# Shorter product waits in the first block's LayerNorm chain, and another start and rate for the second block's convolution, in a one-core encoder block on Trainium2

## The chip, the cores and the metric

The kernel runs on one core of one Trainium2 chip. Its time is the device time of one execution, in microseconds (us). Before the change the median of three runs is 2229.48 us, the lowest 2222.62 and the highest 2231.29. About 0.5%, some 11 us, is what a measurement of this kernel can tell from no change.

## The reference, cut to what matters

One layer of a streaming encoder works on 2048 tokens of 1024 channels. An input projection makes the input of a pooling branch, a pair for a gated linear unit (GLU) and two gates. The branch that this change concerns takes the GLU's output through a causal convolution of width 31 per channel, a LayerNorm over its 512 channels, a swish and a projection; the pooling branch takes means over trailing windows.

```python
def trailing_mean_minus_self(u, window):        # windows 2, 4, 8, 16 by group of 128 channels
    ...
    return (mean - uf).astype(u.dtype)

def pool_mixer(u, pool_w, pool_scale, w_pool_out):
    ...                                         # a 128x128 map for each group
    return mixed @ w_pool_out

def conformer_conv(glu_in, conv_w, conv_b, ln_g, ln_b, w_conv_out):
    a, gate = jnp.split(glu_in, 2, axis=-1)
    v = a * jax.nn.sigmoid(gate)
    v = lax.conv_general_dilated(v, rhs, ...) + conv_b
    v = layernorm(v, ln_g, ln_b)
    v = jax.nn.silu(v)
    return v @ w_conv_out

    merged = jax.nn.sigmoid(g_a) * branch_a + jax.nn.sigmoid(g_b) * branch_b
    x = x + rmsnorm(merged @ w_o[l], norm_mix_post[l])
    h = rmsnorm(x, norm_mlp_pre[l])
    f = jnp.square(jax.nn.relu(h @ w_up[l])) @ w_down[l]
```

## The kernel before, in words

The tokens are worked in two blocks of 1024 (`b` is 0 for block one and 1 for block two). A tile is 128 partitions by 1024 elements, 512 KB. Each large matrix product is split into a high and a low part in fp32r, so that a product of two operands takes three matmul passes, and the projections with eight input chunks go through a scheme with seven products in place of eight: an `Octet` runs products 1 to 7, each of 24 matmuls 128x512, in the order `ORDER`; the first two octets of a group are interleaved by `START`.

**The main line and the lanes.** The order of the products is written out by hand. After each product the program calls `bg()`, which advances the background work: generators in `Lane` objects (line 1423). A lane has a rate, its steps a product: the rate is added to a credit, each step that a generator yields costs one, and a `yield n` ends the turn, clears the credit and leaves out the next n-1 products. What a step issues is tied behind the main line's last marked instruction on each engine (`behind`); within that, a scheduler with priorities lays down one fixed order for each engine and DMA queue when the program is built. So each engine, and SP's DMA queue, works through its list in order: an instruction that waits holds up those behind it.

**The stretch around the change.** Block two's input projection, line 1589, runs 49 products: the pooling input's octet interleaved with GLU's first, then GLU's second, two for gate a (`ga`) and two for gate b (`gb`). Beside it run up to three lanes, called in this order after each product:

- the rest of block one's convolution (`conv_steps(0, ...)`, a scalar-tensor-tensor instruction at line 919 for each of 31 taps and four groups of channels, and an addition into `sums`), then block one's LayerNorm chain `norm_steps(0, 1)`. Its rate is 3.2 and, from the tenth product on, 2.8;
- from the tenth product on, block two's pooling `pool_steps(1, False)` at 1.7 steps a product: for each of four groups the window sums, a scalar-tensor-tensor (line 1027) that is the last read of the window tiles, a split, and the small product `mix`;
- a lane with block two's convolution, which waits until the two others are done.

**The LayerNorm chain** (`norm_steps`, line 934). It splits the sum over the groups (a cast on ScalarE and a subtraction on VectorE), takes the mean on TensorE (`mu`, lines 951 and 952), loads the four convolved tiles back from `yd`, subtracts the mean and stores them, adds the squares, takes their sum over channels on TensorE (line 550, tile `sm`) and the inverse root on VectorE, spreads it (line 645), loads the tiles again, multiplies, applies sigmoid and gain, and stores the result to `zd`.

**What comes next.** After the 49 products the program takes the convolution's lane away, drains the other two, and starts `merge(0)`: `fetch(zd, 0)` loads the four tiles of `zd`, casts them (line 1051) and takes the low parts (a subtraction, line 119), and products `B` multiply them by the convolution's output weights. Block two's convolution goes on beside `merge` (0.5 steps a product), the output projection (6) and the up projection (1.2, later 2.8), and block two's own LayerNorm follows it there.

The tiles live in pools with a fixed number of buffers: 28 of `big`, nine of `tr`, two window tiles `v`, one `y` for the convolution's sum, one `r` and one `sm`, and three accumulators in PSUM for the products.

Of the kernel before, what the change touches and what calls it, by code (L numbers as in the profile page):

```python
# [24 lines left out]
CC = CW // P  # L25
# [35 lines left out]
def f32(ap):  # L61
    return ap.bitcast(F32)
# [3 lines left out]
def block_kernel(  # L66
# [35 lines left out]
    def mk(pl, tag, dt=F32, shape=(P, TB)):  # L102
        return pl.tile(list(shape), dt, tag=tag, name=nm(tag))
# [11 lines left out]
    def add(o, a, b):  # L115
        return nc.vector.tensor_tensor(o, a, b, op=ALU.add)  # L116

    def sub(o, a, b):
        return nc.vector.tensor_tensor(o, a, b, op=ALU.subtract)  # L119

    def mul(o, a, b):
        return nc.vector.tensor_tensor(o, a, b, op=ALU.mult)  # L122

    def load(o, src):
        return nc.sync.dma_start(o, src)  # L125
# [83 lines left out]
    def col(i):  # L209
        return cst[:, i : i + 1]  # L210


    def split(src, pl, tag):
        hi = mk(pl, tag, F32R)
        lo = mk(pl, tag, F32R)
        nc.scalar.copy(hi, src)
        sub(lo, src, f32(hi))
        return hi, lo
# [43 lines left out]
    def matmuls(ps, w, at, rhs, start=True, stop=True, main=True):  # L262

        order = passes(len(rhs))
        for n, (wp, k, xp) in enumerate(order):
            i = nc.tensor.matmul(  # L266
                ps,
                w[wp][:, (at + k) * P : (at + k + 1) * P],
                rhs[k][xp],
                start=start and n == 0,  # L270
                stop=stop and n == len(order) - 1,
                skip_group_check=True,
            )
            if main and n == 0:
                ordered(i)
        return i

    def psum(lab):
        return ps_mm.tile([P, TB], F32, tag="mm", name=nm(lab))
# [383 lines left out]
    def inv_rms_steps(ss, inv_n, tmp, lag, got):  # L663
        st = root_pe(*ss, inv_n=inv_n)
        yield lag
        yield from spread_steps(root_dve(st), tmp, lag, got)
# [33 lines left out]
    def tr(dt=F32):  # L700
        return mk(*TR, dt)
# [5 lines left out]
    def window(n=TB):  # L707
        return mk(p_v, "v", F32, (P, n))
# [183 lines left out]

        return [one(0), one(1)]

    sums = {}

    def conv_steps(b, groups, ahead=True):


        def get(c):  # L900
            v = window(TAPS - 1 + TB)
            load(v, vd[c][:, b * TB : b * TB + TAPS - 1 + TB])
            return v

        v = None
        for c in groups:
            if v is None:
                v = get(c)
                yield 1
            nv = None  # L910
            acc = mk(p_y, "y")
            for k in range(TAPS):
                wk = col(C_CW + c * TAPS + k)
                if k == 0:
                    nc.vector.tensor_scalar(
                        acc, v[:, :TB], wk, col(C_CB + c), op0=ALU.mult, op1=ALU.add
                    )
                else:
                    nc.vector.scalar_tensor_tensor(  # L919
                        acc, v[:, k : k + TB], wk, acc, op0=ALU.mult, op1=ALU.add  # L920
                    )
                if ahead and k == 15 and c != groups[-1]:
                    nv = get(c + 1)
                yield
            v = nv
            if c == 0:
                sums[b] = mk(p_ss, "sm")
                nc.vector.tensor_copy(sums[b], acc)
            else:
                add(sums[b], sums[b], acc)  # L930
            load(yd[b, c, 0], acc)
            yield

    def norm_steps(b, lag):

        yield 3
        sh, sl = split(sums[b], *TR)
        yield 3
        mu = mk(p_ss, "r", F32, (P, W))[:, :TB]
        y = {}  # L940

        def prefetch(c):
            y[c] = tr()
            load(y[c], yd[b, c, 0])

        for c in range(2):
            prefetch(c)
        for t in (0, 1):
            s = slice(t * T, (t + 1) * T)
            rb = mk(ps_rb, "rb", F32, (P, T))  # L950
            nc.tensor.matmul(rb, ones, sh[:, s], start=True, stop=False)
            nc.tensor.matmul(rb, ones, sl[:, s], start=False, stop=True)
            nc.scalar.activation(mu[:, s], rb, AF.Copy, scale=1.0 / CW)
        yield 1
        ss = mk(p_ss, "sm")
        for c in range(CC):
            if c + 2 < CC:
                prefetch(c + 2)
            sub(y[c], y[c], mu)
            load(yd[b, c, 0], y[c])  # L960
            sq = ss if c == 0 else tr()
            nc.scalar.activation(sq, y[c], AF.Square)
            if c % 2:
                yield 1
            if c:
                add(ss, ss, sq)
        yield lag
        r = mk(p_ss, "r", F32, (P, W))[:, :TB]
        halves = [ss[:, t * T : (t + 1) * T] for t in (0, 1)]

        def got(t, rb):
            nc.scalar.copy(r[:, t * T : (t + 1) * T], rb)

        yield from inv_rms_steps(halves, inv_c, TR, lag, got)
        prefetch(0)
        yield 1
        sg = {}
        for c in range(CC + 1):
            if c < CC:
                if c + 1 < CC:  # L980
                    prefetch(c + 1)
                mul(y[c], y[c], r)
                sg[c] = tr()
                nc.scalar.activation(
                    sg[c], y[c], AF.Sigmoid, scale=col(C_LG + c), bias=col(C_LB + c)
                )
                nc.scalar.activation(
                    y[c], y[c], AF.Identity, scale=col(C_LG + c), bias=col(C_LB + c)
                )
            if c:  # L990
                mul(y[c - 1], y[c - 1], sg[c - 1])
                load(zd[b, c - 1, 0], y[c - 1])
            yield 1
# [9 lines left out]
    def pool_steps(b, alone):  # L1003

        def get(g):
            s, u = window(W), tr()
            load(s, ud[g][:, b * TB : b * TB + W])
            load(u, ud[g][:, HALO + b * TB : HALO + b * TB + TB])
            return s, u

        s, u = get(0)
        yield 1
        for g in range(CC):
            w, m = WINDOWS[g], 1
            while m < w:
                lo = HALO - (w - 2 * m)
                s2 = window(W) if alone or m in (2, 8) else mk(p_ss, "r", F32, (P, W))
                add(s2[:, lo:], s[:, lo:], s[:, lo - m : W - m])
                s, m = s2, 2 * m
                yield  # L1020
            if b == 0:
                mul(
                    s[:, HALO : HALO + w],
                    s[:, HALO : HALO + w],
                    cst[:, C_CNT + g * HALO : C_CNT + g * HALO + w],
                )
            nc.vector.scalar_tensor_tensor(
                u, s[:, HALO:], 1.0 / w, u, op0=ALU.mult, op1=ALU.subtract
            )
            hl = split(u, *TR)  # L1030
            if g + 1 < CC:
                s, u = get(g + 1)
            yield 3
            ps = psum("mix")
            for t in (0, 1):
                h = slice(t * T, (t + 1) * T)
                matmuls(ps[:, h], pw, g, [tuple(p[:, h] for p in hl)], main=False)
            o = tr()
            nc.scalar.activation(o, ps, AF.Copy, scale=col(C_PSC + g))
            yield  # L1040
            load(mxd[b, g, 0], o)
            yield
# [407 lines left out]
    lanes = []  # L1450
# [98 lines left out]
    def more():  # L1549
        pool_weight()  # L1550
        tail.gens.append(chain_of(pool_steps(0, True), conv_steps(0, (1, 2, 3), False)))
        tail.rate = 3
# [11 lines left out]
    parts = Parts(lambda ops: input_parts(1, ops))  # L1564
    lanes.clear()
    branch_a(0, mixed, parts.step)
    done = set()

    def marked(gen, k):
        yield from gen  # L1570
        done.add(k)

    def behind_all(gen, *ks):
        while not done.issuperset(ks):
            yield 1
        yield from gen

    rest = [marked(chain_of(*rest), "conv")]
    lanes += [Lane(3.2, *rest, marked(norm_steps(0, 1), "norm"))]

    def pooling():
        lanes[0].rate = 2.8
        lanes.append(Lane(1.7, marked(pool_steps(1, False), "pool")))
        lanes.append(Lane(2.0, behind_all(conv_steps(1, (0, 1, 2, 3)), "conv", "pool")))


    pi = pool_in(1, parts)[0]
    g1 = glu(1, parts), gate(1, parts, 3, sad, "ga", "lows")
    run(
        [then(pooling, pi)],  # L1590
        g1[0],
        g1[1],
# [499 lines left out]
```

## Time and profile before

| | before |
|---|---|
| median of three runs | 2229.48 us |
| lowest, highest | 2222.62, 2231.29 us |
| profiled execution | 2233.46 us |
| its span, first to last instruction | 2231.7 us |
| granted TensorE clock, mean | 0.988 |
| TensorE (PE) busy | 2173.5 us, 97% |
| VectorE (DVE) busy | 1685.3 us, 76% |
| ScalarE (ACT) busy | 1052.1 us, 47% |
| DMA, mean over the span | 255 GB/s |

A row of the timeline has a start in us from the span's start, a duration, the engine (a `q` behind it: its DMA issues), the line, the operation, out<-in by the program's tile names, shapes, a count of merged instructions and, in brackets, the idle time of the engine before it and what ended that. A row of the waits has the waiting instruction, what it waited for, the total, the number of times and the longest. A row of the windows has a stretch, its length, each engine's busy time with its count of instructions, the granted TensorE clock, the share of the DMA engines that was busy and GB/s. A row of the lines has a count, the busy time and the mean of one in ns, and the idle time before. Neighbouring matmuls overlap, so a start-to-start distance says more than a duration.

### The profile page before, as it was taken

How to read it: one execution, taken by the hardware profiler on the slowest of the kernel's cores; microseconds unless marked ns; L12 is line 12 of the kernel's file. 1: busy time of each engine (PE TensorE's matmuls, PEld its weight loads, DVE VectorE, ACT ScalarE, POOL GpSimd, SP SyncE). 2: the span in 40 equal slices, each digit the busy share in tenths (PEclk: the TensorE clock that was granted, in tenths of full speed). 3: DMA queues.
4: the chain of work that ended last, by engine and by line, in shares of the span. 5: the costliest groups of instructions: out<-in, count | busy, mean ns of one | idle time of the engine just before them, and what ended most of it. 6: DMA issues, size and time to landing. Idle time of an engine off the chain costs nothing. (4 is left out here: it accounts for less than half of the span.)

```text
span 2231.7 us, 25071 instructions
## 1 busy us (share of the span) xinstructions
PE 2173.5 (97%) x9576; PEld 1791.4 (80%) x9576; DVE 1685.3 (76%) x1637; ACT 1052.1 (47%) x1094; POOL 27.0 (1%) x51
## 2 busy tenths in 40 slices
PE   9999999999989999999999999999999999999996
PEld 7887888788768888788888877888878888888875
DVE  8897788995779899877757856876744656596667
ACT  6444454334443545455635765655554322224553
POOL 1000000000000000000000000000000000000001
PEclk9999999999999999999999999999999999999997
DMA  7778897777996788335787676995957545446798
GB/s 270 246 266 310 332 337 283 248 253 280 321 335 232 250 336 301 133 142 196 280 298 254 235 274 239 338 327 189 368 203 233 186 161 185 145 145 221 267 311 254
DMA packets 158264, 568.04 MB, mean 255 GB/s; under 512 B 17696, under 2 KB 17952, under 8 KB 158112
## 3 DMA queue, kind: packets, MB, share of 16 engines
q1 hardware_dynamic: 140608, 503.43, 63.7%
q10 hardware_dynamic: 12672, 46.14, 5.3%
q0 software_dynamic: 4864, 16.87, 2.8%
q8 instruction: 75, 1.23, 0.2%
q14 instruction: 45, 0.37, 0.0%
HBM read 378.58 MB, written 188.84 MB: 254 GB/s over the span
## 5 line engine op out<-in xcount | busy, mean ns | idle before, releaser
L266 PE MATMUL up<-big,wh 128*128 128x512 f32 x1792 | 485.1, 393 | 5.6 <-DVE tr L116 3.8
L266 PEld LDWEIGHTS up<-big,wh 128*128 128x128 f32 x1792 | 338.6, 189 | 78.3 <-DVE tr L116 4.6
L223 ACT CAST wh<-wr 128x1024 fp32r<-128x1024 f32 x177 | 185.7, 1051 | 320.9 <-PE up L266 81.5
L266 PE MATMUL down<-tr,wh 128*128 128x512 f32 x800 | 312.9, 391 | 0.0
L919 DVE SCALAR_TENSOR_TENSOR y<-v,cst,y 128x1024 f32<-128x1024 f32 x240 | 307.5, 1281 | 2.8
L266 PE MATMUL down<-fo,wh 128*128 128x512 f32 x784 | 302.7, 391 | 1.2 <-ACT fo L1761 1.2
L266 PE MATMUL up<-big,wl 128*128 128x512 f32 x896 | 277.7, 391 | 0.0
L266 PE MATMUL down<-fo,wl 128*128 128x512 f32 x768 | 238.4, 392 | 2.6 <-DMA wl<-lows 2.6
L223 ACT CAST wh<-ws 128x1024 fp32r<-128x1024 f32 x118 | 124.1, 1051 | 212.1 <-PE up L266 75.1
L266 PEld LDWEIGHTS up<-big,wl 128*128 128x128 f32 x896 | 169.1, 189 | 35.5 <-DVE wl L119 0.4
L116 DVE TENSOR_TENSOR big<-big,down 128x1024 f32<-128x1024 f32 x88 | 107.0, 1219 | 118.5 <-PE down L266 109.3
L1761 ACT CAST fo<-tr 128x1024 fp32r<-128x1024 f32 x86 | 86.7, 1049 | 208.8 <-PE down L266 134.1
L266 PEld LDWEIGHTS down<-tr,wh 128*128 128x128 f32 x800 | 151.0, 189 | 31.2
L119 DVE TENSOR_TENSOR wl<-ws,wh 128x1024 fp32r<-128x1024 f32 x110 | 134.4, 1222 | 53.9 <-ACT wh L223 53.8
L266 PEld LDWEIGHTS down<-fo,wh 128*128 128x128 f32 x784 | 147.7, 188 | 32.2 <-ACT fo L1761 1.7
L266 PEld LDWEIGHTS down<-fo,wl 128*128 128x128 f32 x768 | 145.3, 189 | 33.1 <-DMA wl<-lows 3.0
L119 DVE TENSOR_TENSOR wl<-wr,wh 128x1024 fp32r<-128x1024 f32 x100 | 122.0, 1221 | 27.0 <-ACT wh L223 25.7
L119 DVE TENSOR_TENSOR tr<-tr,fo 128x1024 fp32r<-128x1024 f32 x86 | 101.8, 1221 | 45.2 <-ACT fo L1761 45.1
L266 PE MATMUL glu<-big,wh 128*128 128x512 f32 x464 | 125.0, 391 | 4.4 <-DVE tr L116 2.8
L266 PE MATMUL wo<-big,wh 128*128 128x512 f32 x480 | 128.7, 390 | 0.0
L266 PE MATMUL ga<-big,wh 128*128 128x512 f32 x448 | 120.1, 390 | 3.0 <-DVE tr L116 3.0
L266 PE MATMUL gb<-big,wh 128*128 128x512 f32 x448 | 121.7, 394 | 0.0
(194 smaller groups left out, 3367.7 us busy)
## 6 DMA issues: line engine op xcount, KB each, us to landing
tr<-fd SPq DMA_DIRECT2D x110, 512.0 KB, 4.7
wl<-kept SPq DMA_DIRECT2D x85, 512.0 KB, 4.6
kept<-wl SPq DMA_DIRECT2D x72, 512.0 KB, 5.6
wr<-w_down SPq DMA_DIRECT2D x68, 512.0 KB, 4.7
wr<-w_up SPq DMA_DIRECT2D x64, 512.0 KB, 4.6
wr<-w_in SPq DMA_DIRECT2D x60, 512.0 KB, 4.9
fd<-tr ACTq DMA_DIRECT2D x54, 512.0 KB, 3.5
fd<-tr SPq DMA_DIRECT2D x48, 512.0 KB, 3.1
```

What stands on the lines that cost most here:

```text
L116: return nc.vector.tensor_tensor(o, a, b, op=ALU.add)
L119: return nc.vector.tensor_tensor(o, a, b, op=ALU.subtract)
L223: nc.scalar.copy(hi[:, :n], src[:, :n])
L266: i = nc.tensor.matmul(ps, w[wp][:, (at + k) * P : (at + k + 1) * P], rhs[k][xp], start=start and n == 0, stop=stop and n == len(order) - ...
L919: nc.vector.scalar_tensor_tensor(acc, v[:, k : k + TB], wk, acc, op0=ALU.mult, op1=ALU.add)
L1761: nc.scalar.copy(hi, t)
```

## The change: what it does

Three edits, all of them in the order and pace of background work; no instruction of the computation is added or taken away.

1. In `norm_steps` the two `yield 3` at the start become `yield 1` for block one. Block two keeps 3.
2. The set `done` is made earlier, and `pool_steps` adds the key `("windows", b)` to it right after the last group's line 1027. The lane of block two's convolution now waits for block one's convolution and for that key, in place of the pooling's end.
3. That lane's rate is 1.5 steps a product in place of 2.0 for the rest of the input projection.

```diff
-    sums = {}
+    sums, done = {}, set()
...
     def norm_steps(b, lag):
 
-        yield 3
+        yield 3 if b else 1
         sh, sl = split(sums[b], *TR)
-        yield 3
+        yield 3 if b else 1
...
             nc.vector.scalar_tensor_tensor(
                 u, s[:, HALO:], 1.0 / w, u, op0=ALU.mult, op1=ALU.subtract
             )
+            if g + 1 == CC:
+                done.add(("windows", b))
             hl = split(u, *TR)
...
     branch_a(0, mixed, parts.step)
-    done = set()
-
     def marked(gen, k):
...
         lanes[0].rate = 2.8
-        lanes.append(Lane(1.7, marked(pool_steps(1, False), "pool")))
-        lanes.append(Lane(2.0, behind_all(conv_steps(1, (0, 1, 2, 3)), "conv", "pool")))
+        lanes.append(Lane(1.7, pool_steps(1, False)))
+        lanes.append(Lane(1.5, behind_all(conv_steps(1, (0, 1, 2, 3)), "conv", ("windows", 1))))
```

## The prediction, made before the changed kernel was run

> **What bounds the kernel now.** I read the page first, then who waits for whom on TensorE, then the timeline around the longest waits.
>
> ```profile
> span 2231.7 us, 25071 instructions
> PE 2173.5 (97%) x9576; PEld 1791.4 (80%) x9576; DVE 1685.3 (76%) x1637; ACT 1052.1 (47%) x1094; POOL 27.0 (1%) x51
> ```
>
> TensorE is busy for 2173.5 of 2231.7 us, so all idle time of PE together is 58 us, and no reordering of background work can give more than that, plus what a lowered clock costs beside it. The waits say where it sits:
>
> ```profile
> PE B L266 <- ACT big L1051: 5.1, 2, 3.3
> PE B L266 <- DVE big L119: 4.6, 2, 3.8
> ...
> PE rb L550 <- DVE sm L116: 2.5, 1, 2.5
> ```
>
> The two largest rows belong to one place, the first `B` product of block one's merge, which waits for the cast and the low part of its `zd` tiles; together 9.7 us. The third, 2.5 us, is the LayerNorm chain's own sum over channels. The timeline at the merge, the count of matmuls over 628.75 to 647.1, and two rows that price a product:
>
> ```profile
> 628.31 0.39 PE L266 MATMUL gb<-big,wl 128*128 128x512 f32 x1
> 631.98 0.51 PE L266 MATMUL B<-big,wh 128*128 128x512 f32 x1 [3.27 <-ACT big L1051]
> ...
> 647.15 0.85 PE L266 MATMUL B<-big,wl 128*128 128x512 f32 x3
> ```
>
> ```profile
> L266 PE MATMUL B<-big,wh 128*128 128x512 f32 x14 | 7.5, 652 | 9.7 <-ACT big L1051 5.1 <-DVE big L119 4.6
> L266 PE MATMUL B<-big,wl 128*128 128x512 f32 x4 | 2.0, 601 | 0.0
> ```
>
> ```profile
> 497.99 1.56 PE L266 MATMUL mix<-tr,pw 128*128 128x512 f32 x6
> 499.39 0.86 PE L266 MATMUL ga<-big,wh 128*128 128x512 f32 x3
> ...
> 537.50 1.56 PE L266 MATMUL mix<-tr,pw 128*128 128x512 f32 x6
> ```
>
> Between two of the pooling's small products (`mix`, behind products 27 and 34 of the 49) lie seven undisturbed products of 24 matmuls: (537.50 - 499.39) / 7 = 5.44 us a product, 0.227 us a matmul. At that pace the first `B` could start at 628.31 + 0.23 = 628.54, and the 18 matmuls before 647.15 would take 4.1 us. They took 647.15 - 628.54 = 18.6. **This place loses 14.5 us**: 9.7 of waiting and 4.8 of matmuls that ran slowly between and after the waits.
>
> Why the tiles are late is in the other rows there:
>
> ```profile
> 629.74 0.39 SPq L125 DMA_DIRECT2D zd<-tr  x1
> ...
> 637.05 0.32 SPq L125 DMA_DIRECT2D big<-zd  x1
> ```
>
> ```profile
> 641.28 1.04 ACT L1051 CAST big<-big 128x1024 fp32r<-128x1024 f32 x1 [5.70 <-DMA big<-zd]
> ```
>
> ```profile
> 642.35 1.23 DVE L119 TENSOR_TENSOR big<-big,big 128x1024 fp32r<-128x1024 f32 x1 [3.84 <-ACT big L1051]
> ```
>
> The last tile is stored to `zd` at 629.74, when the gate products are already over; its load is issued at 637.05, the cast starts at 641.28, the low part is there at 643.58. So the end of the LayerNorm chain sets this wait, and the chain is paced by products, which the change alters.
>
> **The first edit, the two shorter waits.** A lane that meets `yield 3` does its next step three products later, with `yield 1` one later. Adding up credits (2.8 a product in the first lane, 1.7 in the pooling's, with the resets at each numbered yield), block one's last convolution step falls behind product 31 of the 49, and so does the pooling's line 1027 of the last group. Before, the split falls behind product 34 and `mu` behind 37; after, behind 32 and 33. Everything later in the chain keeps its distance, so it moves by four products. The row that checks it:
>
> ```profile
> 555.25 0.39 PE L951 MATMUL rb<-tr,ones 128*128 128x512 f32 x1
> ```
>
> `mix` holds PE for 499.39 - 497.99 = 1.40, so product 35 starts at 538.90 and product 37 ends at 538.90 + 3 x 5.44 = 555.2, where `mu` stands, as counted. After the change `mu` comes behind product 33, at 499.39 + 6 x 5.44 = 532.0: 23.2 us earlier (four products, 21.8, and the `mix` it now precedes).
>
> From `mu` at 555.25 to the last low part at 643.58 the chain takes 88.3 us. With the same length it ends at 532.0 + 88.3 = 620.3, and PE reaches `B` at 628.5. That leaves 8.2 us of margin, so the wait at `B` goes: -14.5 us. The four casts, four subtractions and four loads are then hidden under the last two gate products. If that cover fails, each late tile costs again what these rows show. The loads need `big` buffers, which the last `gb` octet's first two products hand back (products 43 and 44, at about 596 and 601); that is early enough. After it the next thing late would be a gate tile for the merge's first multiplication; its loads stand behind the `zd` loads in SP's list and so move forward with them.
>
> Can `mu` be on time?
>
> ```profile
> 526.70 1.22 DVE L116 TENSOR_TENSOR sm<-sm,y 128x1024 f32<-128x1024 f32 x1
> ```
>
> ```profile
> 527.55 1.00 ACT L428 COPY tr<-ga 128x1024 f32<-128x1024 f32 x1
> ...
> 539.92 1.03 ACT L216 CAST tr<-sm 128x1024 fp32r<-128x1024 f32 x1
> ```
>
> The sums end on DVE at 527.92; ACT is free of product 32's copy at 528.55; the cast takes 1.03 and a subtraction 1.23 (the row at 642.35), which gives 530.8 against 532.0. It is on time by 1.2 us, so I cost the shortened waits at nothing here, with the risk below. On ACT the cast starts as soon as the copy ahead of it is done, so the weight casts behind it in ACT's list are held for its 1.03 alone. On PE, products 34 and later stand behind `mu`.
>
> **The second and third edits, start and pace of block two's convolution.** Its load moves on SP's queue from behind product 35 to behind 31, past the weight loads of four products.
>
> ```profile
> 546.27 2.07 SPq L125 DMA_DIRECT2D v<-vd  x1
> ```
>
> ```profile
> 555.12 0.81 DVE L915 TENSOR_SCALAR y<-v,cst 128x1024 f32<-128x1024 f32 x1 [12.91 <-DMA v<-vd]
> ```
>
> ```profile
> 527.90:555.00 27.10, 27.10 (x121) 22.40 (x120) 3.69 (x4) 10.77 (x11) 0.00 (x0) 1.00 0.95 329
> ```
>
> Between 527.90 and 555.00 DVE is busy for 3.69 us of 27.10, so the early steps fall into a hole and cost PE nothing. Before, products 36 to 49 carry 14 x 2 = 28 steps; after, products 32 to 49 carry 18 x 1.5 = 27. The convolution enters the merge one step behind, a line 919 instruction:
>
> ```profile
> L919 DVE SCALAR_TENSOR_TENSOR y<-v,cst,y 128x1024 f32<-128x1024 f32 x240 | 307.5, 1281 | 2.8
> ```
>
> 1.28 us on DVE, and following the later rates (0.5, 6, 1.2, 2.8) the last sum of block two still falls behind the same product of the up projection. Cost nothing. Over the chain's stretch DVE carries half a conv step a product less, which favours the chain slightly; I count nothing for it.
>
> **The chain's own sum over channels.** It waits today:
>
> ```profile
> 577.68 0.39 PE L266 MATMUL gb<-big,wl 128*128 128x512 f32 x1
> 580.55 2.09 PE L550 MATMUL rb<-inv_c,sm 128*128 128x1 f32 x16 [2.48 <-DVE sm L116]
> ```
>
> ```profile
> 174.40 0.93 PE L266 MATMUL ga<-big,wh 128*128 128x512 f32 x3 [2.98 <-DVE tr L116]
> ```
>
> ```profile
> 174.40:178.40 4.00, 4.00 (x18) 3.33 (x19) 4.00 (x6) 0.95 (x1) 0.00 (x0) 1.00 0.37 153
> 582.21:585.63 3.42, 3.42 (x10) 2.75 (x10) 3.42 (x6) 1.06 (x1) 0.00 (x0) 0.50 0.91 329
> ```
>
> It comes 580.55 - 577.91 = 2.64 us late, and the granted clock is 0.50 for the 3.42 us from 582.21, another 1.71: 4.35 in all. A wait of 2.98 us before 174.40 is followed by clock 1.00, so a short wait draws such a stretch at some times and not at others. [...] After the change four products still lie between `mu` and this sum, plus the `mix` of product 34 (1.40), so the wait could fall to 1.2; against that the pooling's last tiles now share the nine `tr` buffers with the chain's loads. I take it as unchanged, 0, with -4.35 (gone) and +4.35 (twice) as bounds.
>
> **The sum.** The profiled execution took 2233.46 us, 4.0 above the median. 2233.46 - 14.5 = 2219.0; on the median, 2229.48 - 14.5 = **2215.0 us**.
>
> **The rivals.** *One: the wait moves to `mu`.* The convolution's first step is now issued in the same turn as the sums' low part. If the fixed order of DVE has it first, the low part waits for that step's load. The load can't be issued before product 31 ends, 499.39 + 4 x 5.44 = 521.2, or, behind what SP then waits for, some 5 us later; it took 555.12 - 546.27 = 8.85; with 0.81 and 1.23 the low part is there at 532.1 to 537.1 against 532.0. Price 0 to 5.1 us, with a slow stretch (1.71) up to 6.8; time up to 2215.0 + 6.8 = 2221.8. For it: DVE stood 12.91 us before just this step. Against: the cast can be ready first. [...]
>
> *Two: the change doesn't do what it says, since the chain is paced by its DMAs.* The chain goes through DRAM three times, and SP's list waits for its landings, here over 520 to 645:
>
> ```profile
> SPq L125 <- DMA zd<-tr: 11.6, 3, 4.8
> ```
>
> Earlier, these three waits stand among the weight loads of `gb` in place of behind them. If DMA latency stretches the chain by more than the margin of 8.2 us, the rest is paid at `B` again. With the 11.6 us added twice, 23.2 - 8.2 = 15.0 and all is lost: 2229.5; with half of that, about 2222. Against: the same DMA share, 0.95, held in the stretch where the chain ran before.
>
> *Three, slower: the removed cover is paid on PE.* `mu`, the sum over channels and the spread stand in PE's list in order. The shortened waits take away 4 x 5.44 = 21.8 us in which PE ran other products. If the chain's own work fills that time, PE waits it out at these three places, with three slow stretches of 1.71: 21.8 + 5.1 - 14.5 = +12.4, 2241.9. It turns slower than before where those waits pass 14.5 us together. Against: `mu` showed no wait, the sum 2.48, the spread none, and by the count above `mu` still has 1.2 us in hand.
>
> **How the numbers follow.** Forecast 0.58, rival one 0.20, two 0.14, three 0.08. A measurement of this kernel tells about 0.5% from no change, 11.1 us, so faster means below 2218.3. The forecast lies 3.3 us beyond that, and the three runs spread over 8.7 us (2222.62 to 2231.29), so I give it 0.8 of its chance there: 0.46. Rival one has a quarter of its chance there, 0.05. Faster 0.51; slower is rival three, 0.08; the same is the rest, 0.41. The low end takes the sum's wait away too, 2215.0 - 4.35, less 1.6 for the spread of runs: 2209.0. The high end is no gain at all, 2229.5; above it lies rival three, below the low end little.
>
> **What would show it.** Right: no wait of `B` over about 1 us, `mu` about 23 us earlier on PE, the `zd` stores done before 612, clock 1.00 through the merge, and `v<-vd` issued near 522 to 526. Rival one: a wait of L951 on DVE, with a conv step before the low part. Two: `B` still waits on casts that wait for `zd`. Three: waits at L951, L550 and L645 that sum to more than 14.5. Wrong altogether: `B` starts without a wait and the time doesn't fall, which would mean that a later stage takes the time back.

## The result and the profile after

| | before | after |
|---|---|---|
| median of six runs each | 2229.64 us | 2217.44 us |
| lowest, highest | 2222.62, 2234.97 | 2212.93, 2220.66 |
| ratio, 95% interval | | 0.9939 [0.9921, 0.9956] |
| profiled execution | 2233.46 us | 2218.92 us |
| its span | 2231.7 us | 2217.1 us |
| granted TensorE clock, mean | 0.988 | 0.991 |

The change is 12.2 us or 0.61% faster by the medians (14.5 us by the two profiled executions, of which the one before ran 3.8 us over its median and the one after 1.5). Two further measurements of the unchanged pair on other chips, `after2` and `after3` below, gave 0.9931 and 0.9919.

The page of the kernel after, its head:

```profile
span 2217.1 us, 25074 instructions
PE 2166.1 (98%) x9576; PEld 1786.1 (81%) x9576; DVE 1686.0 (76%) x1637; ACT 1052.7 (47%) x1094; POOL 27.3 (1%) x51
```

PE is busy for 7.4 us less than before, with the same 9576 matmuls. The lowered clock is of that size: 0.012 x 2231.7 = 26.8 us lost to it before, 0.009 x 2217.1 = 20.0 after, some 7 us less (the shares are rounded to a thousandth, about 1 us each way). The other 7.2 us of the 14.6 by which the span is shorter is idle time of PE. Over the stretch from 500 to 720 us the kernel after has one wait on TensorE in the waits view, and it is not one of the three of before:

```profile
PE gb L266 <- DMA wl<-kept: 2.0, 1, 2.0
```

The timeline of TensorE, kernel after, at `mu`, at the chain's sum over channels (L550) and where block one's merge begins:

```profile
534.10 0.39 PE L951 MATMUL rb<-tr,ones 128*128 128x512 f32 x1
...
558.20 1.84 PE L550 MATMUL rb<-inv_c,sm 128*128 128x1 f32 x16
...
629.98 0.39 PE L266 MATMUL gb<-big,wl 128*128 128x512 f32 x1
630.21 1.52 PE L266 MATMUL B<-big,wh 128*128 128x512 f32 x6
631.57 0.84 PE L266 MATMUL B<-big,wl 128*128 128x512 f32 x3
632.25 0.61 PE L266 MATMUL B<-big,wh 128*128 128x512 f32 x2
```

The first `B` stands 0.23 us behind the last `gb`, one matmul's pace, with no bracket: the wait is gone, and so are the slow matmuls, as the windows view over the stretch that lost 14.5 us before shows (clock 1.00, PE busy throughout):

```profile
628.54:647.15 18.61, 18.61 (x84) 15.41 (x83) 17.14 (x15) 7.23 (x7) 0.00 (x0) 1.00 1.02 384
```

To compare executions that start a few us apart, I take a stretch from the first `ga` matmul behind the small product `mix` of product 27 to the first output projection matmul (`wo`). Its rows, first before (its start, 499.39, is in the prediction), then after:

```profile
686.61 0.62 PE L266 MATMUL wo<-big,wh 128*128 128x512 f32 x2
```

```profile
501.43 0.39 PE L266 MATMUL ga<-big,wh 128*128 128x512 f32 x1
...
673.73 0.39 PE L266 MATMUL wo<-big,wh 128*128 128x512 f32 x1
```

That is 187.22 us before and 172.30 after, 14.9 less. Ahead of it the execution after is 2.0 us later, and behind it 1.7 us shorter.

### The profile page after: what moved, and what is told of

Read it like the earlier page. It is cut to its first block, busy times and chain, and to the rows that moved or that the text cites. A ratio compares the mean times of both kernels' runs of the same rounds, so it can differ in the third digit from the quotient of the medians.

```text
span 2217.1 us, 25074 instructions
## 1 busy us (share of the span) xinstructions
PE 2166.1 (98%) x9576; PEld 1786.1 (81%) x9576; DVE 1686.0 (76%) x1637; ACT 1052.7 (47%) x1094; POOL 27.3 (1%) x51
## 5 line engine op out<-in xcount | busy, mean ns | idle before, releaser
L919 DVE SCALAR_TENSOR_TENSOR y<-v,cst,y 128x1024 f32<-128x1024 f32 x240 | 307.4, 1281 | 2.8
L116 DVE TENSOR_TENSOR big<-big,down 128x1024 f32<-128x1024 f32 x88 | 106.9, 1219 | 115.5 <-PE down L266 107.0
```

Source lines behind the costliest of these rows:

```text
L919: nc.vector.scalar_tensor_tensor(acc, v[:, k : k + TB], wk, acc, op0=ALU.mult, op1=ALU.add)
```

## The experiments

All numbers of the table are read from each kernel's profiled execution, times from the start of the stretch just defined; the ratio is against the kernel before on the same chip. "Sum's wait" is that of L550; "half clock" is the time lost to the lowered clock in the stretch, half of its duration.

| kernel | ratio [95%] | stretch | `mu` | waits of the first `B` product | sum's wait | half clock |
|---|---|---|---|---|---|---|
| before | 1 | 187.2 | 55.9 | 9.7 | 2.5 | 6.8 |
| `before2` | one execution, 2233.6 us | 187.5 | 55.9 | 9.2 | 2.6 | 8.5 |
| after | 0.9939 [0.9921, 0.9956] | 172.3 | 32.7 | 0 | 0 | 1.7 |
| `after2` | 0.9931 [0.9912, 0.9951] | 170.1 | 32.7 | 0 | 0 | 0 |
| `after3` | 0.9919 [0.9903, 0.9935] | 170.2 | 32.7 | 0 | 0 | 0 |
| `norm_only` | 0.9953 [0.9935, 0.9971] | 172.2 | 32.7 | 0 | 0.8 | 1.7 |
| `norm_only2` | 0.9946 [0.9927, 0.9965] | 178.0 | 32.7 | 0 | 2.2 | 5.1 |
| `conv_only` | 1.0003 [0.9991, 1.0016] | 188.1 | 55.9 | 10.1 | 2.4 | 10.2 |
| `norm_early` | 0.9955 [0.9942, 0.9967] | 168.7 | 32.7 | 0 | 0 | 0 |
| `yield5` | 1.0068 [1.0043, 1.0093] | 195.3 | 77.6 | 20.9 | 0 | 13.7 |
| `yield2` | 0.9959 [0.9946, 0.9972] | 174.8 | 45.0 | 1.0 | 0.6 | 1.7 |
| `yield0` | 0.9931 [0.9917, 0.9944] | 173.1 | 30.2 | 0 | 1.3 | 1.7 |
| `aside` | 0.9942 [0.9924, 0.9960] | 173.5 | 32.7 | 0 | 0.9 | 1.7 |
| `aside_yd` | 0.9920 [0.9904, 0.9935] | 169.0 | 32.7 | 0 | 0 | 0 |

A profiled execution need not be a typical one: that of `norm_only` is the fastest of its ten (2212.04 us, median 2221.94), that of `yield5` the fastest of its four.

**Each half by itself.** `norm_only` is the kernel before with edit 1 alone (the key of edit 2 is added in it too, but no lane reads it); `conv_only` has edits 2 and 3 alone; `norm_early` has edits 1 and 2, with the old rate.

`norm_only` against the kernel before, at both places:

```diff
-        yield 3
+        yield 3 if b else 1
```

`conv_only` against the kernel after, at both places:

```diff
-        yield 3 if b else 1
+        yield 3
```

`norm_early` against the kernel after:

```diff
-        lanes.append(Lane(1.5, behind_all(conv_steps(1, (0, 1, 2, 3)), "conv", ("windows", 1))))
+        lanes.append(Lane(2.0, behind_all(conv_steps(1, (0, 1, 2, 3)), "conv", ("windows", 1))))
```

> Edit 1 alone: the two waits of block one's LayerNorm chain are one product, the convolution of block two starts behind the pooling's end at 2.0 as before. Theory (the wait at B goes because the chain's end moves four products, 21.8 us, forward): no wait of B over 1 us, mu near 534, and nearly the whole gain: ratio 0.992 to 0.996. Rival (the earlier start and lower pace of the convolution free VectorE for the chain, and that is what brings the zd tiles in time): B still waits 4 us or more and the ratio is over 0.997.

> Edits 2 and 3 alone: the chain's waits stay three products, the convolution starts behind the pooling's last window read at 1.5 steps a product. Theory: mu stays near 555 to 557, the last zd tile is still loaded after 635, B waits 8 to 11 us in all as before and the ratio is 0.998 to 1.002. Rival (lower VectorE load shortens the chain itself): the chain from mu to the last low part falls from 88 us to under 80 and B's wait falls below 4 us, ratio under 0.997.

> Edits 1 and 2 with the old pace of 2.0. Theory: the pace is of no weight for the time; no wait at B, ratio within 0.002 of the full change's 0.994, and 36 convolution steps in place of 27 done by the end of the input projection. Rival (the lower pace is needed, since VectorE then holds up the chain): the sum over channels at L550 or the loads of gb wait 2 us or more longer than in the full change, or B waits again, and the ratio is over 0.997.

Measured on one chip: `norm_only` 2221.94 us, `conv_only` 2233.20, `norm_early` 2222.20, before 2233.07. The waits of TensorE between 500 and 720 us, first of `norm_only`:

```profile
PE rb L550 <- DVE sm L116: 0.8, 1, 0.8
PE gb L266 <- DMA wl<-kept: 0.6, 1, 0.6
```

and of `conv_only`:

```profile
PE B L266 <- ACT big L1053: 6.8, 2, 3.5
PE B L266 <- DVE big L119: 3.3, 2, 2.8
PE rb L550 <- DVE sm L116: 2.4, 1, 2.4
```

The two rows of `B` stand or fall with edit 1. Edits 2 and 3 alone bring nothing, and the chain from `mu` to the last low part is as long there as before (89.3 us against 88.3).

`norm_early` has the shortest stretch of all and no wait of TensorE between 500 and 720 us, so the lower rate isn't needed there. Its time isn't better. What follows the stretch took 1549.3 us in its profile against 1541.9 to 1545.9 in the three of the full change, and the largest wait there is the up projection's, 7.1 us against 4.2 in the kernel after:

```profile
PE up L266 <- DVE tr L116: 7.1, 3, 3.6
```

That fits a gain given back later; I made no experiment on that later wait, so this is argued, not shown.

**The number of products waited.** With the same two lines, 5, 2 and 0 in place of 3 and 1:

`yield5` against the kernel before, at both places:

```diff
-        yield 3
+        yield 3 if b else 5
```

`yield2` and then `yield0` against the kernel after, at both places:

```diff
-        yield 3 if b else 1
+        yield 3 if b else 2
```

```diff
-        yield 3 if b else 1
+        yield 3 if b else None
```

> The kernel before with waits of five products in place of three: the chain starts four products later, so that its last steps fall behind the last product and are issued at once. Theory (the chain's end sets the start of B): mu near 577, B's wait grows from 9.7 by 10 to 22 us and the time by about that, ratio 1.005 to 1.012. Rival (B waits for something else of the same moment, its loads from zd or the gates): B's wait stays under 13 us, ratio under 1.003.

> The full change with waits of two products in place of one: the chain moves two products (10.9 us) forward in place of four. Theory: the last low part at about 643.6 - 10.9 = 632.7 while the ninth matmul of B would need it at 630.4, so B waits about 2 us in place of 9.7 and the ratio is 0.993 to 0.997. Rival (the wait goes only where the whole margin is there, since all of the chain's DMAs then lie before the gate's last weight loads): B waits over 5 us and the ratio is over 0.997.

> The changed kernel with no wait at all at the two places of block one's chain: split and mu both fall behind product 32. In the changed kernel's profile product 32 ends at 528.7, the sums end on VectorE at 529.8 and their low part at 532.8. Theory (the product waits are cover, and below one product the rest is paid on TensorE): mu waits for the low part 3 to 5 us, with a slow stretch of 1.7 at times, and the ratio is 0.001 to 0.003 above after3's. Rival (TensorE's fixed order moves mu back behind the next product): no wait of L951 over 0.5 us and the ratio is within 0.001 of after3's.

Measured: `yield5` 2244.10 us (before 2230.32 on that chip), `yield2` 2222.49 (2233.07), `yield0` 2219.78 (2234.93). The dose reads straight off the waits. `yield5`, TensorE between 500 and 720 us:

```profile
PE B L266 <- ACT big L1051: 18.9, 3, 14.0
PE B L266 <- DVE big L119: 2.1, 4, 0.7
```

and the first rows of the merge in the timeline of `yield2`:

```profile
631.88 1.37 PE L266 MATMUL B<-big,wh 128*128 128x512 f32 x5
633.82 0.50 PE L266 MATMUL B<-big,wh 128*128 128x512 f32 x1 [0.58 <-DVE big L119]
...
635.71 0.50 PE L266 MATMUL B<-big,wh 128*128 128x512 f32 x1 [0.47 <-DVE big L119]
```

With five products `B` waits 20.9 us in place of 9.7 and the kernel is 0.68% slower. The chain starts 21.8 us later there and the wait grows by only 11.2, since the chain is shorter, 655.21 - 580.19 = 75.0 us in place of 88.3: its last steps are drained behind the last product and wait for no more products. With two products the chain keeps its length (635.66 - 547.36 = 88.3) and PE catches up with its end: two waits of half a us. So two products in place of one are almost enough, and the change itself has a little in hand.

In `yield0` the expected wait did not come. I looked for it at `mu`, which had 1.2 us in hand. There was none: the fixed order laid `mu` inside product 33 (which starts at 500.33 + 5 x 5.44 = 527.5 there and, with the four matmuls of `mu` in it, ends at about 534; `mu` stands at 530.50) rather than in front of it, so that it came only 2.5 us earlier than in the kernel after. Waits came at two later places, the sum over channels and a `gb` product:

```profile
PE rb L550 <- DVE sm L116: 1.3, 1, 1.3
PE gb L266 <- ACT tr L1041: 0.6, 1, 0.6
```

The experiment therefore says nothing on what a late `mu` would cost; that its ratio, 0.0012 above that of `after3`, lies in the range expected is luck.

**The new wait.** The kernel after has a wait of `gb` for a weight load that wasn't there before. SP's issues in the timeline of after, and the row of TensorE:

```profile
550.14 3.42 SPq L125 DMA_DIRECT2D yd<-tr  x2
...
559.66 0.87 SPq L125 DMA_DIRECT2D wl<-kept  x2
```

```profile
568.97 0.97 PE L266 MATMUL gb<-big,wl 128*128 128x512 f32 x3 [2.02 <-DMA wl<-kept]
```

The weight load stands behind the chain's stores to `yd` in SP's list: issued at 559.66, needed at 566.95. SP's longest waits between 545 and 562 us:

```profile
SPq L125 <- ACT wh L223: 7.1, 3, 2.5
SPq L125 <- DMA sad<-tr: 2.4, 2, 2.1
SPq L125 <- DMA tr<-yd: 1.4, 1, 1.4
SPq L125 <- DVE tr L119: 1.2, 1, 1.2
```

A store waits for VectorE, but for 1.2 us only. More goes on two loads of `wr` between the stores and the weight load (556.18 and 559.24), which wait for ScalarE's casts. To test the place I sent the stores of block one's chain through GpSimd's queue: both kinds in `aside`, the `yd` stores alone in `aside_yd`. The edit of both against the kernel after:

```diff
-            load(yd[b, c, 0], y[c])
+            (load if b else aside)(yd[b, c, 0], y[c])
```

and in `aside` alone also

```diff
-                load(zd[b, c - 1, 0], y[c - 1])
+                (load if b else aside)(zd[b, c - 1, 0], y[c - 1])
```

> The changed kernel with block one's chain storing its eight tiles (yd and zd) from GpSimd's queue in place of SP's. Theory one (the wl load was late since the chain's stores, which wait for VectorE, stood before it in SP's in-order list): the wait of gb for wl<-kept goes, ratio 0.001 to 0.002 below after2's. Rival (it was late since the DMA engines were full there, share 1.00 from 545 to 560, and took 9.2 us to land): the wait stays at 1 to 4 us and the ratio is within 0.001 of after2's.

> The changed kernel with only the four yd stores of block one's chain on GpSimd's queue. Theory: the wait of gb for wl<-kept near 569 goes and the wait of gb for VectorE near 622 (2.2 us with both kinds of stores moved) doesn't come; ratio 0.001 to 0.002 below after3's, the fastest version. Rival: one of the two waits is there and the ratio is within 0.001 of after3's.

Measured: `aside` 2217.61 us beside 2217.05 for the unchanged `after2` on that chip; `aside_yd` 2217.07 beside 2216.93 for `after3`. The waits between 500 and 720 us, first of `aside`, then of `aside_yd`:

```profile
PE gb L266 <- DVE tr L116: 2.2, 1, 2.2
PE rb L550 <- DVE sm L116: 0.9, 1, 0.9
```

```profile
PE gb L266 <- DMA wl<-kept: 0.4, 1, 0.4
```

The place is confirmed. Without the stores in front of it the weight load is issued at 551.27 in `aside` and at 554.39 in `aside_yd`, 51.5 and 51.8 us behind the start of the stretch in place of 58.2, and the wait is gone in both. The 0.4 us of `aside_yd` belong to another load, near 613 us. What the stores' own wait for VectorE cost isn't shown: without them the fixed order puts the weight load in front of the two loads of `wr` too. The time isn't better: `aside` gets a wait of the same size for VectorE, and `aside_yd`, whose stretch is 1.1 us shorter than the unchanged kernel's at its best, is level with it. A microsecond here is below what these runs can tell.

**Repeats.** `before2`, `after2` and `after3` are the two kernels unchanged, `norm_only2` is `norm_only` again.

> The kernel before, unchanged, for a second profile. Theory: the loss at B is of the fixed order and repeats: 8 to 11 us of waiting, and up to 5 us of slow matmuls beside it, of which the slow part depends on where the halved clock falls.

> The changed kernel once more, for a second profile and beside the next kernel on one chip. Theory: B starts without a wait again, mu behind product 33, ratio 0.992 to 0.996; the wait for wl<-kept behind the chain's sum (2.0 us in the first profile) comes back at the same place, 1 to 4 us, if it lies in the fixed order of SP's list, and is absent if it was an accident of that execution.

> The changed kernel once more, as the standard for the three others on one chip. Theory: ratio 0.992 to 0.996.

> Edit 1 alone once more, beside the full change. Theory (the whole gain is edit 1's): ratio within 0.002 of after3's. Rival (the convolution's earlier start and lower pace add some of their own, since after3's chain runs beside fewer steps): ratio more than 0.002 above after3's, with waits at the sum over channels or at gb that after3 doesn't have.

Measured: 2233.60, 2217.05, 2216.93 and 2224.01 us. `before2` has the loss at `B` again (9.15 us of waiting). On one chip the full change (four runs, 2214.5 to 2220.15) lies below edit 1 alone (six runs, 2214.24 to 2228.26) by 7 us of the medians, more than was expected if the whole gain were edit 1's (0.0027 of the ratio, not under 0.002), but the ratios' intervals overlap, 0.9903 to 0.9935 and 0.9927 to 0.9965. Both profiles of edit 1 alone have a wait of the sum over channels, 0.8 and 2.2 us with half clock (0.50) behind it, and the three of the full change have none. That edits 2 and 3 add 0.1 to 0.3% on top of edit 1 is suggested by this, not settled. How the sum's way is cleared can be read on VectorE, where the subtractions of the mean wait for their loads from `yd`. The two longest such waits of `norm_only2`:

```profile
550.41 1.23 DVE L119 TENSOR_TENSOR tr<-tr,r 128x1024 f32<-128x1024 f32 x1 [3.82 <-DMA tr<-yd]
...
556.82 1.23 DVE L119 TENSOR_TENSOR tr<-tr,r 128x1024 f32<-128x1024 f32 x1 [4.04 <-DMA tr<-yd]
```

and the only one of the kernel after:

```profile
551.98 1.23 DVE L119 TENSOR_TENSOR tr<-tr,r 128x1024 f32<-128x1024 f32 x1 [0.47 <-DMA tr<-yd]
```

Between 534 and 560 us these waits add up to 8.8 and 10.1 us in the two profiles of edit 1 alone, and to 0.5, 1.3 and 0.4 in the three of the full change, where the last of the four loads is issued about 3 us earlier. `norm_early` has no wait of the sum either (1.9 us for these loads), so the lower rate isn't needed for it. Why the loads come earlier in SP's list I did not follow.

## Why the prediction was right, and where its terms were off

The forecast was 2215.0 us, the median is 2217.44; on the profiled execution 2219.0 was forecast and 2218.92 taken. That these last two agree to 0.1 us is luck: of the terms below, 4.35 us gained and 3.7 lost were not in the sum, and the parts outside the stretch, 2.0 us longer and 1.7 shorter, cancel too. Point by point:

- **The wait at `B`: right in place and size.** It goes with edit 1 alone and grows with the waits (1.0, 9.7 and 20.9 us for two, three and five products).
- **`mu` 23 us earlier: right.** 55.86 us behind the start of the stretch before (555.25 - 499.39), 32.67 after (534.10 - 501.43), 23.2 less. It didn't wait.
- **The margin of 8.2 us: mis-sized, and nearly the step that failed.** From `mu` to the last low part the chain took 630.97 - 534.10 = 96.9 us, not 88.3 (94.5 and 94.7 in `after2` and `after3`). The rows of SP, VectorE and ScalarE after:

```profile
608.95 0.38 SPq L125 DMA_DIRECT2D zd<-tr  x1
...
617.43 1.43 SPq L125 DMA_DIRECT2D big<-zd  x3
```

```profile
629.74 1.23 DVE L119 TENSOR_TENSOR big<-big,big 128x1024 fp32r<-128x1024 f32 x1 [0.25 <-ACT big L1053]
```

```profile
628.65 1.05 ACT L1053 CAST big<-big 128x1024 fp32r<-128x1024 f32 x1 [0.79 <-DMA big<-zd]
```

  Up to the last store nothing is longer: 608.95 - 534.10 = 74.9 us, before 629.74 - 555.25 = 74.5. Then the last load is issued at 618.5, 9.5 us behind that store in place of 7.3, and it lands 10.1 us later in place of 4.2. In the windows view these are the landings, first before, then after:

```profile
637.05:641.28 4.23, 3.47 (x8) 1.68 (x6) 1.46 (x2) 0.00 (x1) 0.00 (x0) 0.62 0.95 337
```

```profile
618.50:628.65 10.15, 10.15 (x47) 8.40 (x46) 8.63 (x8) 6.12 (x6) 0.00 (x0) 1.00 1.03 417
```

  Three loads were issued together, into DMA engines that were full (share 1.03, 417 GB/s). This is the mechanism of rival two, DMAs that stretch the chain, though not at the waits that it priced: no wait of SP for a `zd` store to land is left between 520 and 645 us, 11.6 us of them before. What the prediction held against it, that the DMA share stays at 0.95, failed: from that store to the last landing the share is 1.00. So the margin was used up as the prediction counted it: the last low part is there 0.8 us after the first `B` has started. PE doesn't wait all the same, since that low part isn't needed at once. In `yield2` it is the eleventh `B` matmul that waits for it; here the eleventh starts at 632.25 + 0.23 = 632.48, 1.5 us after it. `yield2` shows what the other side of that edge looks like.
- **The sum over channels, taken as unchanged: mis-sized.** Its 2.64 us and the 1.71 of slow clock went, the lower bound given (-4.35).
- **A term not in the sum: the new wait of `gb`.** 2.02 us and 1.71 of half clock, +3.7. The prediction saw that the chain's DMAs would move in among the weight loads of `gb`, but counted only what this does to the chain, not what the chain does to the weights. The terms add up: -14.5 - 4.35 + 3.7 = -15.1, against 14.9 less of the stretch. In `after2` this wait is 1.49 us with no slow clock, in `after3` 0.65, with 0.67 more for another weight load at 612.23.
- **Edits 2 and 3 at nothing: held for those two alone** (1.0003); on top of edit 1 see the repeats.
- **Rival one** had the convolution's first step ahead of the low part on VectorE. The load was issued at 524.04, as forecast, but the order was the other one:

```profile
531.57 1.23 DVE L119 TENSOR_TENSOR tr<-sm,tr 128x1024 fp32r<-128x1024 f32 x1 [1.76 <-ACT tr L216]
532.72 0.81 DVE L915 TENSOR_SCALAR y<-v,cst 128x1024 f32<-128x1024 f32 x1
```

  So whether the low part would have waited behind that step was not put to the test. Elsewhere in the profile of before a waiting instruction did hold up the next one on VectorE. L919 below reads a window tile that had landed at 93.2 us and a sum last written at 104.1, and it started only behind the L116 that waited 3.43 us for TensorE:

```profile
110.63 1.23 DVE L116 TENSOR_TENSOR tr<-pool,tr 128x1024 f32<-128x1024 f32 x1 [3.43 <-PE pool L266]
111.77 1.28 DVE L919 SCALAR_TENSOR_TENSOR y<-v,cst,y 128x1024 f32<-128x1024 f32 x1
```

- **Rival three** needed waits at L951, L550 and L645. In the stretch the kernel after has none of them, and `yield0` only one, of 1.3 us.

## What to carry to other kernels

When a chain of background work ends just behind its deadline, its start can be moved by whole steps of the main line, and the count of steps gave the new place almost to the tenth of a microsecond in every kernel here but `yield0`, where the fixed order put it elsewhere. In the kernel after, the chain's length carried over up to its last store only; price the loads behind it by the DMA share of the stretch that it moves into (here the last one took 10.1 us to land at a share of 1.03, and 4.2 at 0.95 before). A moved step also moves its stores and loads in the issue queue, so look for what stands behind them there (here a weight load). Once the large wait is gone, stop at the small ones: taking away the wait for the weights gave no time that could be measured in two experiments, of which one brought another wait of the same size.

## What the runs showed of the hardware

The prediction left open why one short wait of TensorE draws half clock and another doesn't. In the profiles of before and after, the start and end of all slow stretches, the end of the program's last one apart, lie on one grid of 3.41 us in each. Before, for instance, they begin or end at 582.21, 585.62, 633.41, 640.24, 643.65 and 647.06: 1, 14, 2, 1 and 1 steps of 3.413. Between 120 and 700 us I laid this grid over the two timelines and counted in each of its windows that ran at full clock the time without a matmul of many columns; L550's matmuls on one column count as idle. In four windows it was 2.02 us or more (3.41, 2.91 and 2.62 before, 2.02 after), and the next window was at half clock each time; in the other 331 it was 1.83 us or less, and the next never was. With L550 counted as busy, the 3.41 us (the window from 578.80) would be 1.75, less than the 1.83 that drew nothing. This is a count over two profiles, and four windows give no exact boundary. Two pairs of rows of the windows view. In the kernel after, the window before the slow stretch and the slow one itself:

```profile
566.75:570.16 3.41, 1.39 (x6) 1.01 (x6) 3.11 (x10) 0.61 (x1) 0.00 (x0) 1.00 0.92 315
```

```profile
570.20:573.62 3.42, 3.42 (x9) 2.64 (x8) 0.00 (x0) 0.00 (x0) 0.00 (x0) 0.51 0.63 253
```

In the kernel before, the two windows across which the wait of 2.98 us before 174.40 lies:

```profile
172.60:176.02 3.42, 1.62 (x7) 1.40 (x8) 3.42 (x5) 1.06 (x1) 0.00 (x0) 1.00 0.59 242
169.19:172.60 3.41, 2.24 (x10) 1.50 (x8) 3.41 (x4) 1.04 (x1) 0.00 (x0) 1.00 1.02 416
```

PE is busy for 1.39 of 3.41 us in the first, and half clock follows (0.51); the longer wait is split, 1.79 us in one window and 1.2 in the other, and the 3.41 us from 176.02 ran at 1.00. So 2.02 us inside one window drew half clock, and 2.98 us across two drew none. In `yield2` 0.56 us drew it, with the 1.8 us of one-column matmuls behind it in the same window:

```profile
573.34 1.95 PE L550 MATMUL rb<-inv_c,sm 128*128 128x1 f32 x16 [0.56 <-DVE sm L116]
```

```profile
575.90:579.32 3.42, 3.42 (x9) 2.65 (x8) 1.22 (x1) 0.00 (x0) 0.00 (x0) 0.50 0.33 129
```

The wait of `ga` near 174 us is there in the kernel after too, 2.96 us long and up to 175.35; the grid splits it into 1.83 and 1.13 us, and the clock stays at 1.00 again. So in these profiles what a wait of 2 to 3 us cost beside itself, nothing or 1.71 us, went with where it lay on that grid, whose first line stands 1.95 us behind the span's start before and 0.14 after. After 700 us, where other small matmuls run, the same count doesn't part the windows cleanly (before, 1.68 us drew half clock and 1.74 didn't); what counts as busy there I haven't found out.
